# Weight-sum DMAs of the first down product: eight of 48 asked for two tiles earlier, and a lower rate behind the half-size tiles

## The chip, the core and the metric

The kernel runs on one core of a Trainium2 chip. The metric is the time of one execution on the device in microseconds (us); with several runs of a kernel, their median. All data are float32. TensorE multiplies matrices into PSUM banks, VectorE and ScalarE do the elementwise work, GpSimd (POOL in the profile) does little but issue DMAs that copy or accumulate in DRAM, and SyncE (SP) issues the DMAs that load weights. Each of the two has a DMA queue of its own in the profile (q0 for GpSimd, q1 for SyncE), and both move their bytes with the same 16 DMA engines.

## What is computed

One layer of a streaming encoder on 512 tokens of width 1024:

```python
x = x + 0.5 * swiglu_ffn(rmsnorm(x, g1), w_gate1, w_up1, w_down1)   # hidden width 2816
x = x + hybrid_mixer(rmsnorm(x, gm), ...)                           # attention and pooling
x = x + 0.5 * swiglu_ffn(rmsnorm(x, g2), w_gate2, w_up2, w_down2)
x = rmsnorm(x, gf)

def swiglu_ffn(x, w_gate, w_up, w_down):
    return (silu(x @ w_gate) * (x @ w_up)) @ w_down
```

The change lies in the first feed-forward block, whose two halves are called the up stage (gate and up products and SiLU) and the down product.

## The kernel before

**Precision.** Each float32 operand is split into a high and a low part (`split`, L128; ScalarE writes the high part, VectorE the low), and each product is three TensorE products (`mm3`, L173 to L178).

**The up stage** (`ffn_up`, L383) works through 22 feature tiles of 128 hidden features, numbered here in their order, 0 to 21. Tiles 0 to 4 (`PLAIN` = 5) are full-size: each takes 2 x 8 products of 128x512, with weights loaded by `weights` (L163). Tiles 0 and 1 are made together from the first four loads (L406 to L420) and then evacuated from PSUM by `evacuate` (L393), which scales, applies SiLU, multiplies gate and up into the activations and returns the tile `sg` that held the SiLU. Tiles 2 and 3 follow in the loop at L492, and tile 4 at L506 to L528.

Tiles 5 to 21 are half-size (loop at L550): a Strassen-like scheme replaces eight half-size products by seven, each of 4 x 3 TensorE products of 128x256. It needs sums and differences of weight blocks, which VectorE makes (`sum13`, `sum24`, `low...`) and ScalarE splits (`high...`, L444). From L548 the order of TensorE, VectorE, ScalarE and SyncE is as written in the code (`manual_schedule`); before that a scheduler places the instructions. In tile n, SyncE fetches the weights of tile n + 2 with two DMAs of 512 KB (`fetch`, L431: L436 and L437, tensor `in_wA`), into one of two raw buffers, which VectorE's last reader of tile n has just freed. Behind that ScalarE splits the first block of tile n + 1 (`high11`, L574, executed at L444), which the second DMA (L437) of the fetch made one tile earlier brings. Behind it, in ScalarE's order, stands the copy of a PSUM bank (`copy(z[:, HT:], up_hi, -1.0)`, L580, executed at L540) that must be done before TensorE writes that bank again (L584).

**The weight sums.** The down product uses the same scheme, and its sums of weight blocks (T1 to T4, for 6 groups of rows) are made in DRAM ahead of time by GpSimd's queue: `Down.steps` (L646) lists 48 DMAs, 24 that copy a block to `wsum` (from the weights `in_wB`, or from another `wsum`) and 24 that accumulate a second block onto it. Most of them move 512 KB, those of the last group 256 KB. An accumulation can only be issued when the copy beneath it has landed, a copy from another `wsum` only when that one is complete. They are issued in the order of the list.

**What paces them.** `make_sums(after, n)` (L669) takes the next steps from the list. It copies one column of the tile `after` to a mark (L675), which makes GpSimd wait until that tile is written, and then issues the steps (L677). The number is taken from `rates`, given where `down1` is made (L800 to L801): four behind each of tiles 2, 3 and 4, three behind each of the next six, two behind each of the next nine. It is called in the loop at L501, at L528, and once in each half-size tile (L586, behind VectorE's L585). The GpSimd part of the code is in written order as well, except that marks can be placed ahead of steps that still wait.

The down product reads the sums from L704 on, first at 216.6 us of the profiled execution. The second feed-forward block uses the same functions with `loaded=True`, its own object `down2` and no rates.

Of the kernel before, what the change touches and what calls it, by code (L numbers as in the profile page):

```python
# [23 lines left out]
KH = KF // 2  # L24
# [15 lines left out]
PLAIN = 5  # L40
# [13 lines left out]
def layer(  # L54
# [50 lines left out]
    def temp(dtype=F32):  # L105
        return tpool.tile([P, S], dtype, tag="t", name=name("t"))

    def bank(tag="mm", bufs=4):
        return ps.tile([P, S], F32, tag=tag, name=name(tag), bufs=bufs)
# [63 lines left out]
    def mm3(acc, a, b, start, stop, further=False):  # L173

        more = dict(skip_group_check=True) if further else {}
        nc.tensor.matmul(acc, a[0], b[0], start=start, stop=False, **more)  # L176
        nc.tensor.matmul(acc, a[0], b[1], start=False, stop=False, **more)  # L177
        nc.tensor.matmul(acc, a[1], b[0], start=False, stop=stop, **more)  # L178

    def cut(pair, lo, n):  # L180
        if isinstance(pair[0], list):
            pair, lo = [z[lo // S] for z in pair], lo % S
        return pair[0][:, lo : lo + n], pair[1][:, lo : lo + n]
# [199 lines left out]
    def ffn_up(norm, wA, down, loaded):  # L383
# [9 lines left out]
        def evacuate(f, gate, up):  # L393
            g = temp()
            nc.vector.tensor_tensor(g, gate, norm.rb, op=ALU.mult)
            sg = temp()
            nc.scalar.activation(sg, g, AF.Silu)

            nc.vector.tensor_tensor(sg, sg, norm.rb, op=ALU.mult)
            down.place(f, up, sg)  # L400
            down.sums(f)
            return sg

        consts = constants()
        first = [bank() for _ in range(4)]
        for kp in range(KD // 2):  # L406
# [10 lines left out]
            for kk in range(2):  # L417
                k = 2 * kp + kk
                for j in range(4):
                    mm3(first[j], cut(w, (kk * 4 + j) * P, P), norm.h[k], k == 0, k == KD - 1)  # L420
        evacuate(0, first[0], first[1])
        evacuate(1, first[2], first[3])
        aside = [
            down.pool.tile([P, 6 * groups[g][1] * HT], F32, tag=f"acts{groups[g][0]}", name=name("aside"))
            for g in (G - 3, G - 2, G - 1)
# [80 lines left out]
        n, f = PLAIN - 1, down.order[PLAIN - 1]  # L506
# [41 lines left out]
        with tc.manual_schedule(engines={E.PE, E.DVE, E.Activation, E.SP}):  # L548
            last_silu = last_place = last_sums = nothing
            for n in range(PLAIN, KF):  # L550
                f = down.order[n]
                acc, up_lo, up_hi = bank()[:, :HT], bank()[:, :HT], abank()[:, :HT]
                u, z, sg = temp(), temp(), temp()
# [238 lines left out]
    def block2(i, g):  # L792
# [4 lines left out]
    KPS = (2, 3, 0, 1)  # L797
    order1 = [0, 1, KH, KH + 1] + [f + KH * j for f in range(2, KH) for j in range(2)]
    down1 = Down(
        order1, lambda f: (f % KH, f // KH), block1, [4] * (PLAIN - 2) + [3] * 6 + [2] * 9  # L800
    )  # L801
    down2 = Down(list(range(KF)), lambda f: (f // 2, f % 2), block2)

    with tc.tile_pool(name="act1", bufs=1, reuse_waits="tile") as apool:
        down1.begin(apool)
        ffn_up(n1, wA1, down1, loaded=False)
        p1, p5, p6 = whole(bank), whole(bank), whole(abank)

# [615 lines left out]
    with tc.tile_pool(name="act2", bufs=1, reuse_waits="tile") as apool:  # L1424
        down2.begin(apool)

        for half in range(2):
            for t in range(NT):
# [6 lines left out]
                nc.scalar.copy(z, tp)  # L1435
                nc.sync.dma_start(x_d[half * NT + t], z)
        ffn_up(n3, wA2, down2, loaded=True)
        xt = [hpool.tile([P, S], F32, tag="h", name=name("xt")) for _ in range(2 * NT)]
        rooms.extend((xpool, f"x{i}", 1, 2 * S) for i in range(KD // 2))
# [212 lines left out]
```

## Time and profile before

| what | value |
|---|---|
| median of 3 runs | 864.71 us (863.97 to 865.85) |
| profiled execution, time on the device | 865.0 us |
| its span from first to last instruction | 863.2 us |
| granted TensorE clock | 0.998 |
| GpSimd's DMA queue q0 | 22656 packets, 46.14 MB, 24.7% of the DMA engines' time |
| SyncE's DMA queue q1 | 49088 packets, 110.93 MB, 36.8% |
| up stage of the first block: full-size tiles | about 5 to 65 us |
| up stage of the first block: half-size tiles | about 65 to 236 us |

How to read it: the page gives busy times of each engine over the whole span and in slices; a row of the table by stage gives them for one stretch, with the granted clock, the busy share of the DMA engines (which can exceed 1, as packets overlap) and the GB/s. A row of a timeline gives the start, the duration, the engine, the source line (often that of a helper), the operation and its tiles; a bracket at the end tells how long the engine stood idle just before it, and what ended that idle time. Times are from the start of the span.

### The profile page before, as it was taken

What the parts mean: (1) busy time and instruction counts of PE and PEld (TensorE: products, weight loads), DVE (VectorE), ACT (ScalarE), POOL (GpSimd) and SP (SyncE); (2) the same over time, 40 slices, a digit from 0 to 9 for tenths busy, and PEclk for the clock granted to TensorE, in tenths of its full rate; (3) what the DMA queues carried; (4) which work ended last, traced back from release to release, by engine and by line L of the source; (5) the groups of instructions that cost most, each with busy time, mean ns of one, the idle gap of its engine ahead of it and who ended that gap; (6) DMA issues with size and microseconds to landing.
All of it is one profiled execution on the core that took longest, in us unless ns stands there. A gap on an engine that the chain in (4) does not pass through costs nothing.

```text
span 863.2 us, 14110 instructions
## 1 busy us (share of the span) xinstructions
PE 848.8 (98%) x5296; PEld 757.5 (88%) x5296; DVE 708.3 (82%) x1115; ACT 501.1 (58%) x859; POOL 120.1 (14%) x196
## 2 busy tenths in 40 slices
PE   9999999999999999989999999999999999999996
PEld 7889999999988888867878788889999999988885
DVE  7999898898897769685878667969888898887896
ACT  7445555555676556548647756445555555566573
POOL 0124322222000000120011000102112111122000
PEclk9999999999999999999999999999999999999999
DMA  8199998877576764322212026248778778899832
GB/s 291 57 285 248 293 277 207 202 206 165 144 242 204 254 212 136 97 86 85 75 57 90 25 73 244 80 140 228 212 231 202 189 199 209 251 328 341 274 109 98
DMA packets 72244, 158.50 MB, mean 184 GB/s; under 512 B 6112, under 2 KB 29168, under 8 KB 71792
## 3 DMA queue, kind: packets, MB, share of 16 engines
q1 hardware_dynamic: 49088, 110.93, 36.8%
q0 software_dynamic: 22656, 46.14, 24.7%
q8 instruction: 41, 0.67, 0.3%
q10 hardware_dynamic: 432, 0.54, 0.2%
q14 instruction: 27, 0.22, 0.1%
HBM read 153.38 MB, written 50.34 MB: 236 GB/s over the span
## 4 chain that ended last, share of the span: by engine, by line
PE 91%; DVE 3%; DMA 2%; ACT 2%; issue 1%; SPq 0%; ACTq 0%; DVEq 0%
PE mm L176 22%; PE mm L177 21%; PE mm L178 21%; PE a L176 7%; PE a L177 7%; PE a L178 7%; DMA raw<-in_wA_dram 2%; PE a L1172 1%; PE a L1226 1%; PE a L1214 1%; DVE t L1093 1%; DVE wlo L449 1%; ACT prob L1153 1%; PE a L211 0%; PE a L1431 0%
## 5 line engine op out<-in xcount | busy, mean ns | idle before, releaser
L132 DVE TENSOR_TENSOR wlo<-raw,whi 128x1024 fp32r<-128x1024 f32 (+2 forms) x115 | 125.0, 1096 | 20.7 <-ACT whi L131 20.4
L131 ACT CAST whi<-raw 128x1024 fp32r<-128x1024 f32 (+2 forms) x115 | 106.9, 944 | 57.7 <-PE mm L177 15.5
L177 PE MATMUL mm<-ha,whi 128*128 128x256 f32 x408 | 115.6, 283 | 0.0
L178 PE MATMUL mm<-ha,wlo 128*128 128x256 f32 x408 | 115.0, 282 | 0.0
L176 PE MATMUL mm<-ha,whi 128*128 128x256 f32 x408 | 115.0, 282 | 0.0
L540 ACT ACTIVATE t<-mm 128x256 f32<-128x256 f32 x102 | 39.2, 384 | 121.5 <-PE mm L178 120.8
L449 DVE TENSOR_TENSOR wlo<-wsum,whi 128x1024 fp32r<-128x1024 f32 x68 | 83.0, 1220 | 14.1 <-ACT whi L444 14.1
L178 PEld LDWEIGHTS mm<-ha,wlo 128*128 128x128 f32 x408 | 77.4, 190 | 0.0
L176 PEld LDWEIGHTS mm<-ha,whi 128*128 128x128 f32 x408 | 77.2, 189 | 0.1
L177 PEld LDWEIGHTS mm<-ha,whi 128*128 128x128 f32 x408 | 77.2, 189 | 0.1
L176 PE MATMUL mm<-hhi,whi 128*128 128x512 f32 x192 | 76.0, 399 | 0.0
L177 PE MATMUL mm<-hlo,whi 128*128 128x512 f32 x192 | 75.7, 395 | 0.0
L178 PE MATMUL mm<-hhi,wlo 128*128 128x512 f32 x192 | 74.8, 392 | 0.0
L677 POOL DMA_DIRECT2D wsum<-in_wB_dram x72 | 70.4, 1147 | 11.7 <-issue 8.5
L444 ACT CAST whi<-wsum 128x1024 fp32r<-128x1024 f32 x68 | 67.9, 1048 | 4.1 <-PE mm L177 3.9
L177 PE MATMUL mm<-wlo,ah 128*128 128x512 f32 x176 | 68.6, 390 | 0.0
L178 PE MATMUL mm<-whi,ah 128*128 128x512 f32 x176 | 68.5, 389 | 0.0
L176 PE MATMUL mm<-whi,ah 128*128 128x512 f32 x176 | 68.4, 390 | 0.0
L675 POOL COPY mark<-t 128x1 f32<-128x1 f32 x40 | 15.1, 377 | 382.1 <-DVE t L585 228.0
L449 DVE TENSOR_TENSOR wlo<-raw,whi 128x512 fp32r<-128x512 f32 x68 | 62.5, 951 | 3.4 <-ACT whi L444 3.4
L444 ACT CAST whi<-raw 128x512 fp32r<-128x512 f32 x68 | 56.3, 828 | 11.4 <-DMA raw<-in_wA_dram 6.9
L132 DVE TENSOR_TENSOR ah<-acts,ah 128x512 fp32r<-128x512 f32 (+1 forms) x72 | 45.7, 641 | 14.5 <-ACT ah L131 14.2
(211 smaller groups left out, 2381.5 us busy)
## 6 DMA issues: line engine op xcount, KB each, us to landing
raw<-in_wA_dram SPq DMA_DIRECT2D x87, 512.0 KB, 5.5
wsum<-in_wB_dram POOLq DMA_DIRECT2D x60, 512.0 KB, 7.7
raw<-wsum SPq DMA_DIRECT2D x40, 512.0 KB, 4.4
raw<-in_wB_dram SPq DMA_DIRECT2D x30, 512.0 KB, 4.7
wsum<-wsum POOLq DMA_DIRECT2D x20, 512.0 KB, 5.8
x<-in_xT_dram SPq DMA_DIRECT2D x16, 256.0 KB, 5.7
raw<-in_wQK_dram SPq DMA_DIRECT2D x8, 512.0 KB, 3.5
raw<-in_wO_dram SPq DMA_DIRECT2D x8, 512.0 KB, 3.4
```

The lines of the kernel that those rows point to most:

```text
L131: nc.scalar.copy(hi, src)
L132: nc.vector.tensor_tensor(lo, src, hi.bitcast(F32), op=ALU.subtract)
L176: nc.tensor.matmul(acc, a[0], b[0], start=start, stop=False, **more)
L177: nc.tensor.matmul(acc, a[0], b[1], start=False, stop=False, **more)
L178: nc.tensor.matmul(acc, a[1], b[0], start=False, stop=stop, **more)
L444: nc.scalar.copy(hi, src)
L449: nc.vector.tensor_tensor(lo, src, hi.bitcast(F32), op=ALU.subtract)
L540: nc.scalar.activation(dst, src, AF.Copy, scale=scale)
L675: nc.gpsimd.tensor_copy(mark, after[:, 0:1])
L677: nc.gpsimd.dma_start(self.rows(i, g), self.rows(self.terms[i][at], g), **(dict(accum_op=ALU.add) if at else {}),)
L1093: nc.vector.tensor_tensor(q3, q3, rs[:, t, :].unsqueeze(2).to_broadcast([P, 8, HD]), op=ALU.mult)
L1153: nc.scalar.activation(p, p, AF.Copy, scale=rt)
```

## The change

The steps of the first down product are also asked for behind tiles 0 and 1, four each, and the rates become four behind each of tiles 0, 1 and 2, three behind each of tiles 3 and 4, and two behind each of the next fifteen (half-size) tiles. The sum is 48 as before. The second block is not touched, since `loaded` is true there.

```diff
-        evacuate(0, first[0], first[1])
-        evacuate(1, first[2], first[3])
+        for f in range(2):
+            sg = evacuate(f, *first[2 * f : 2 * f + 2])
+            if not loaded:
+                down.make_sums(sg, 2)
...
     down1 = Down(
-        order1, lambda f: (f % KH, f // KH), block1, [4] * (PLAIN - 2) + [3] * 6 + [2] * 9
+        order1, lambda f: (f % KH, f // KH), block1, [4] * 3 + [3] * (PLAIN - 3) + [2] * 15
     )
```

The functions `evacuate` and `make_sums` themselves are unchanged.

## The prediction, made before the changed kernel was run

> **What bounds the kernel now.** I read the first part of the page, then the table by stage around the change, then who waits for whom there, and last the rows of ScalarE and of the queues in order of time. The page:
>
> ```profile
> span 863.2 us, 14110 instructions
> PE 848.8 (98%) x5296; PEld 757.5 (88%) x5296; DVE 708.3 (82%) x1115; ACT 501.1 (58%) x859; POOL 120.1 (14%) x196
> ```
>
> TensorE is busy for 98% of the span, so a change that moves only DMAs can win only where TensorE stands still for a DMA. The busy time by stage (PE, PEld, DVE, ACT, POOL, granted clock, DMA share, GB/s) shows where that could be:
>
> ```profile
> 30.00:41.00 11.00, 11.00 (x50) 9.13 (x49) 11.00 (x16) 4.12 (x6) 2.25 (x2) 1.00 0.00 0
> 41.00:66.00 25.00, 25.00 (x126) 21.30 (x126) 23.99 (x33) 13.39 (x20) 8.42 (x10) 1.00 0.89 253
> 77.00:87.00 10.00, 9.74 (x83) 9.54 (x81) 7.56 (x10) 4.98 (x9) 3.09 (x4) 1.00 1.09 314
> 87.00:97.00 10.00, 9.54 (x81) 9.55 (x82) 8.70 (x12) 5.87 (x12) 4.97 (x6) 1.00 1.11 318
> ```
>
> From 30 to 41 us no byte is moved, from 41 us on the DMA engines are full, and TensorE loses its first time behind them, after 77 us. The waits from 60 to 125 us (us in total, times, longest) name the chain:
>
> ```profile
> ACT whi L444 <- DMA raw<-in_wA_dram: 4.7, 3, 2.2
> PEld a L176 <- ACT t L540: 1.5, 2, 0.9
> ```
>
> ScalarE waits for the second weight DMA of a half-size tile (L437) to split its first block (L444, `high11`). Behind it in ScalarE's queue stands the copy L540 that frees the PSUM bank `up_hi`, and TensorE waits for that copy. How much that costs is read from the cadence. The last L540 copy of each tile, and the L444 that waits:
>
> ```profile
> 69.67 0.39 ACT L540 ACTIVATE t<-mm 128x256 f32<-128x256 f32 x1 [2.45 <-PE mm L178]
> 79.64 0.39 ACT L540 ACTIVATE t<-mm 128x256 f32<-128x256 f32 x1 [2.45 <-PE mm L178]
> 86.50 0.62 ACT L444 CAST whi<-raw 128x512 fp32r<-128x512 f32 x1 [2.17 <-DMA raw<-in_wA_dram]
> 90.56 0.38 ACT L540 ACTIVATE t<-mm 128x256 f32<-128x256 f32 x1 [2.88 <-PE mm L178]
> 96.05 0.62 ACT L444 CAST whi<-raw 128x512 fp32r<-128x512 f32 x1 [0.77 <-DMA raw<-in_wA_dram]
> 100.50 0.39 ACT L540 ACTIVATE t<-mm 128x256 f32<-128x256 f32 x1 [2.45 <-PE mm L178]
> 107.00 0.62 ACT L444 CAST whi<-raw 128x512 fp32r<-128x512 f32 x1 [1.75 <-DMA raw<-in_wA_dram]
> 111.09 0.39 ACT L540 ACTIVATE t<-mm 128x256 f32<-128x256 f32 x1 [2.92 <-PE mm L178]
> 150.99 0.39 ACT L540 ACTIVATE t<-mm 128x256 f32<-128x256 f32 x1 [2.45 <-PE mm L178]
> 220.80 0.39 ACT L540 ACTIVATE t<-mm 128x256 f32<-128x256 f32 x1 [2.45 <-PE mm L178]
> ```
>
> Undisturbed, a tile takes (220.80 - 150.99) / 7 = 9.97 us. The tile that ends at 90.56 took 10.92 (0.95 lost), the one at 111.09 took 10.59 (0.62 lost), the two beside them 9.97 and 9.94. Late fetches cost 0.95 + 0.62 = 1.57 us here. That is the ceiling of what this change can win: 0.18% of 865.0. Everywhere else that the change touches, TensorE is already without gaps.
>
> **What moves.** The 48 weight-sum DMAs of the first down product keep their order. Asked for so far, behind full-size tiles 0 to 4 and then half-size tiles 5, 6, 7: before 0, 0, 4, 8, 12, 15, 18, 21; after 4, 8, 12, 15, 18, 20, 22, 24. From tile 10 on both stand at 30 and go on in twos. In the compiled order TensorE, VectorE, ScalarE and SyncE keep every instruction in place; GpSimd gets two more mark copies (of 128 elements), and VectorE and ScalarE get one more wait on GpSimd each, for a temporary that tile 4 takes over from a marked one. Tile 4's temporaries are written after 62 us and these marks are read before 40 us, so I cost the waits at nothing; they would count only if GpSimd ran over 20 us late, and its waits below are of 3 us.
>
> The mark copies stand in a stretch where VectorE has no idle time. A copy there and the queue's first DMAs:
>
> ```profile
> 29.89 0.68 DVE L399 TENSOR_TENSOR t<-t,rb 128x512 f32<-128x512 f32 x1
> 38.75 2.25 POOL L675 COPY mark<-t 128x1 f32<-128x1 f32 x1 [36.95 <-DVE t L399]
> 36.87 1.22 DVE L343 TENSOR_TENSOR aside<-aside,aside 128x1024 f32<-128x1024 f32 x1
> 39.74 1.22 DVE L343 TENSOR_TENSOR aside<-aside 128x1024 f32<-128x1024 f32 x1
> 45.70 1.97 POOL L677 DMA_DIRECT2D wsum<-in_wB_dram  x2 [3.09 <-DMA wsum<-in_wB_dram]
> 54.05 0.51 POOL L677 DMA_DIRECT2D wsum<-wsum  x1 [2.51 <-DMA wsum<-in_wB_dram]
> 61.64 0.69 DVE L132 TENSOR_TENSOR ha<-aside,ha 128x512 fp32r<-128x512 f32 x1 [0.67 <-PE mm L177]
> ```
>
> Tile 0's mark becomes ready at 30.57 instead of 38.69 for tile 2's, so the queue starts about 8 us earlier. GpSimd pays at most 2 x 2.25 us more, which nobody but the queue waits for. If a mark held VectorE for its whole 2.25 us, VectorE would have the 0.67 us idle at 61.64 against it; between 0 and 2 x 2.25 us I take 0, since the same addition (L343) takes 1.22 us before the mark at 36.87 and beside it at 39.74. Each accumulation waits until the copy beneath it has landed (the 3.09 and 2.51 us), so the early start is partly spent in waiting.
>
> **Work in the two queues.** Mean rates: accumulations alone (73 to 76 us), copies alone (43 to 45), a weight fetch alone (129.2 to 131.4):
>
> ```profile
> DMA packets 578, 0.59 MB, mean 197 GB/s; under 512 B 18, under 2 KB 576, under 8 KB 577
> DMA packets 190, 0.71 MB, mean 356 GB/s; under 512 B 16, under 2 KB 16, under 8 KB 190
> DMA packets 280, 0.63 MB, mean 285 GB/s; under 512 B 17, under 2 KB 17, under 8 KB 280
> ```
>
> A step of 0.52 MB is 2.66 us as an accumulation and 1.47 us as a copy; a tile's 1.05 MB fetch is 3.7 us. Three steps per half-size tile are on average 6.2 us, with the fetch 9.9 us in a tile of 9.97: a backlog never clears. Two steps are 4.1 + 3.7 = 7.8 us: 2.1 us of a backlog go away per tile. That is the gain. The fetches and what they met:
>
> ```profile
> 43.19 0.61 SPq L437 DMA_DIRECT2D raw<-in_wA_dram  x1
> 66.83 0.55 SPq L437 DMA_DIRECT2D raw<-in_wA_dram  x1
> 74.25 0.61 ACT L444 CAST whi<-raw 128x512 fp32r<-128x512 f32 x1
> 75.86 10.56 DMA raw<-in_wA_dram
> 96.74 10.18 DMA raw<-in_wA_dram
> DMA to landing us min/median/max: 4.4/6.4/10.6
> ```
>
> The two that cost time took 10.56 and 10.18 us; the median of L437 is 6.4. Taking off the losses, a fetch may take 10.56 - 0.95 = 9.61 or 10.18 - 0.62 = 9.56 us before TensorE stops. One has less: tile 7's fetch, issued at 66.83. Its deadline is one tile ahead of tile 8's, 75.86 + 9.61 - 9.97 = 75.50, so 8.67 us. Before, it met an empty queue (ScalarE at 74.25 did not wait). After, 15 steps lie ahead of it, 9 copies and 6 accumulations, 13.2 + 16.0 us, and two fetches, 7.4 us: 36.6 us of work, with 33 us from the first packets at about 34 us, less the waits on landings. So 4 us or more are left over when it starts, and tile 4's three steps (two copies and a half-size one, 3.7 us) come in beside it. Its time lies between the median 6.4 and 10.56; I take 9.5, nearer to the loaded end, since its queue is loaded. That stops TensorE for 9.5 - 8.67 = 0.8 us at about 76 us. The stop gives the next fetch 0.8 us more room (9.6 + 0.8 = 10.4 against the loaded 10.2): no loss. The backlog shrinks by 2.1 us per tile, so tile 10's fetch, which cost 0.62, meets a nearly empty queue.
>
> The Trainium skill (DMA: Bandwidth & Descriptors, "Queues, rings and completion order") says that a DMA engine takes turns between its queue rows, packet by packet. The 10.56 and 10.18 us beside a lightly loaded 6.4 agree: what slows a fetch would be whether the other queue has anything, not how much. That speaks against this change: by it the sum would be that of case C below.
>
> **Sum.** -1.57 (stops removed) + 0.8 (new stop) = -0.8 us: the 865.0 of the profiled execution (its span is 863.2, and 1.8 us lie around it) becomes 864.2. The median, 864.71, lies 0.3 below that execution, within the spread of the three runs (863.97 to 865.85); from it the sum gives 863.9. I predict 864.0, between the two. A difference under 0.2% (1.7 us) is about what a measurement of this kernel cannot tell from none.
>
> **Rivals.**
> A: every fetch lands in time (tile 7's under 8.67 us). For: two steps need only 7.8 of 9.97 us. Against: the load before 66 us. -1.57, 863.1 from the median. Chance 0.24.
> B, my forecast: one smaller stop, earlier. Gain 0.3 to 1.3. Chance 0.40.
> C: the change does not do what it says, the stops only move one tile ahead. Where the fetch takes turns with a queue that is not empty, fetches 7 to 9 take 10.2 us and more, however few steps stand behind: 10.2 - 8.67 = 1.5 us, as much as goes. Change 0, 864.7 (-0.3 to +0.5). Chance 0.22. The rule of the Trainium skill quoted above would have this as long as the other queue has work.
> D, slower: tile 5's fetch, issued at 43.19, now falls among accumulations. ScalarE's split that waits for it starts at 50.41, 7.2 us after the issue; at 10.2 us it starts at 53.4, and VectorE's half, now at 52.30, right behind it at 54.0, 1.7 later. VectorE's only reserve up to 66 us is the 0.67 at 61.64, so it frees the raw buffer 1.0 us later and tile 7's fetch leaves at 67.9; at 10.2 it lands at 78.1, 2.6 behind its deadline. 2.6 - 1.57 is +1.0 us: 865.7. At 11.4 us, two thirds of an accumulation more, it would be 866.9. It decides once tile 5's fetch takes over 8.5 us (52.30 less the split's 0.62 is 51.7), and shows in full once it takes over 9.2:
>
> ```profile
> 50.41 0.62 ACT L444 CAST whi<-raw 128x512 fp32r<-128x512 f32 x1 [2.03 <-DMA raw<-in_wA_dram]
> 52.30 0.68 DVE L449 TENSOR_TENSOR wlo<-raw,whi 128x512 fp32r<-128x512 f32 x1
> ```
>
> Chance 0.14.
>
> **Numbers.** Faster by over 0.2% needs 863.0 or less, below A's 863.1, so only a part of A, where the median hid longer stops than the profiled execution: 0.08. Slower by over 0.2% needs 866.4, the upper half of D and a little of C: 0.09. Within: 0.83. The range goes from A (863.1) to D (865.7) with the sum's rounding: 863.0 to 865.8.
>
> **What would show it.** Right: weight-sum DMAs between 32 and 43 us; no L444 wait over 1 us after 95 us; half-size tiles of 9.97 us from the third on; one tile of about 10.8 that ends near 80 us. Wrong: all tiles 9.97 (A), two or three tiles over 10.4 (C), VectorE's L449 at 52.30 moved past 53 (D). A time outside the range would mean that the change reaches a stage where I saw no cover missing.

## The result

| | the changed kernel | the kernel before, same chips |
|---|---|---|
| median of 21 runs each | 867.58 us (865.03 to 869.79) | 865.05 us (863.97 to 866.78) |
| ratio of the two | 1.0024 (95% interval 1.0016 to 1.0032) | |
| profiled execution, its span | 869.31 us, 867.5 us | 865.0 us, 863.2 us |
| granted clock of the profiled execution | 0.996 | 0.998 |

The changed kernel is slower, by about 2 us; the forecast was 864.0 in a range of 863.0 to 865.8, no difference or a slight gain. The page of the changed kernel (two lines are added in its code, so L449 is L451, L540 is L542, L675 is L677):

```profile
span 867.5 us, 14116 instructions
PE 850.4 (98%) x5296; PEld 759.0 (87%) x5296; DVE 708.0 (82%) x1115; ACT 500.9 (58%) x859; POOL 124.2 (14%) x198
```

Of the 4.3 us that the span grew, TensorE's busy time has 1.6 with the same 5296 matmuls, and idle time the rest. A larger busy time for the same instructions asks for a look at the clock. The table by stage of the changed kernel (columns as before: PE, PEld, DVE, ACT, POOL, granted clock, DMA share, GB/s):

```profile
30.00:41.00 11.00, 11.00 (x50) 9.12 (x49) 11.00 (x16) 4.01 (x5) 4.47 (x6) 1.00 0.56 135
41.00:66.00 25.00, 24.79 (x121) 20.82 (x119) 22.16 (x31) 11.61 (x18) 15.38 (x13) 1.00 1.01 278
77.00:87.00 10.00, 7.77 (x53) 7.57 (x53) 5.21 (x10) 2.65 (x6) 2.91 (x4) 0.83 1.09 301
...
82.00:88.00 6.00, 6.00 (x41) 6.00 (x41) 4.45 (x7) 2.47 (x4) 1.34 (x2) 0.75 1.16 258
...
98.00:108.00 10.00, 10.00 (x86) 10.00 (x85) 9.51 (x16) 5.60 (x11) 1.17 (x3) 1.00 0.55 200
```

The DMAs do start early (share 0.56 from 30 to 41 us instead of 0.00), and from 98 us on the load is light, as intended. Between the two, TensorE loses over 2 us from 77 to 87 us, and from 82 to 88 us the granted clock is 0.75 on average: in the trace's record of the clock it is 0.5 for 3.413 us from 81.64 on. TensorE's rows there show both, a stop and then matmuls of 0.41 us that take 0.28 at full clock:

```profile
65.51 0.28 PE L178 MATMUL a<-xa,wlo 128*128 128x256 f32 x1
67.09 0.39 PE L176 MATMUL mm<-xa,whi 128*128 128x256 f32 x1 [1.29 <-ACT t L542]
...
78.36 0.28 PE L178 MATMUL mm<-xa,wlo 128*128 128x256 f32 x1
80.87 0.38 PE L176 MATMUL a<-ha,whi 128*128 128x256 f32 x1 [2.23 <-ACT t L542]
...
82.34 0.41 PE L176 MATMUL a<-ha,whi 128*128 128x256 f32 x1
...
85.09 0.28 PE L177 MATMUL mm<-ha,whi 128*128 128x256 f32 x1
```

Matmuls start 0.12 us apart when nothing stops them, so the first stop costs 67.09 - 65.51 - 0.12 = 1.46 us and the second 80.87 - 78.36 - 0.12 = 2.39. (The idle time in the bracket is 0.28 less than the distance of the starts, for a matmul is counted busy for 0.28. The expectations below give stops by the distance of the starts.) ScalarE's rows, the split that waits for a fetch and the last copy of each tile:

```profile
54.78 0.62 ACT L446 CAST whi<-raw 128x512 fp32r<-128x512 f32 x1 [5.99 <-PE mm L178]
...
71.57 0.39 ACT L542 ACTIVATE t<-mm 128x256 f32<-128x256 f32 x1 [2.40 <-PE mm L178]
...
79.92 0.62 ACT L446 CAST whi<-raw 128x512 fp32r<-128x512 f32 x1 [3.69 <-DMA raw<-in_wA_dram]
80.72 0.38 ACT L542 ACTIVATE t<-mm 128x256 f32<-128x256 f32 x1
85.53 0.38 ACT L542 ACTIVATE t<-mm 128x256 f32<-128x256 f32 x1 [4.44 <-PE mm L178]
...
95.47 0.39 ACT L542 ACTIVATE t<-mm 128x256 f32<-128x256 f32 x1 [2.45 <-PE mm L178]
...
105.44 0.39 ACT L542 ACTIVATE t<-mm 128x256 f32<-128x256 f32 x1 [2.45 <-PE mm L178]
...
115.42 0.39 ACT L542 ACTIVATE t<-mm 128x256 f32<-128x256 f32 x1 [2.45 <-PE mm L178]
```

By the cadence of the prediction, the tile that ends at 85.53 took 13.96 us, 3.99 over the usual 9.97: 2.39 of the stop and 1.60 of the half clock. All later tiles take 9.94 to 9.98. So the stops of before (1.57) are gone, and the account of the profiled execution is -1.57 + 1.46 + 2.39 + 1.60 = +3.9, beside some 0.4 that it was already behind at 43 us (tile 5's fetch issued at 43.60 instead of 43.19), together the 4.3.

What was late? The chain of work (start, duration, what) of the changed kernel in this stretch, and GpSimd's rows:

```profile
64.41 0.69 DVE t L395
...
68.59 0.35 SPq L438
68.99 10.85 DMA raw<-in_wA_dram
79.96 0.48 issue
80.44 0.39 ACT t L542
```

```profile
36.01 1.97 POOL L679 DMA_DIRECT2D wsum<-in_wB_dram  x2 [2.45 <-DMA wsum<-in_wB_dram]
42.41 0.51 POOL L679 DMA_DIRECT2D wsum<-wsum  x1 [4.43 <-DMA wsum<-in_wB_dram]
...
52.98 0.52 POOL L679 DMA_DIRECT2D wsum<-wsum  x1 [4.66 <-DMA wsum<-in_wB_dram]
...
59.01 0.50 POOL L679 DMA_DIRECT2D wsum<-wsum  x1 [3.54 <-DMA wsum<-in_wB_dram]
59.50 5.04 POOL L677 COPY mark<-t 128x1 f32<-128x1 f32 x1
64.48 3.12 POOL L679 DMA_DIRECT2D wsum<-in_wB_dram  x3
```

Two fetches are late. Tile 5's, issued at 43.60, lands after 11.1 us, and ScalarE splits only at 54.78 (50.41 before; the row names a matmul as what ended the idle time, but the landing, at 54.7, came last). VectorE's part follows (55.44 instead of 52.30), VectorE reaches tile 4's evacuation late (L395 at 64.41 instead of 62.25), and TensorE stops for the bank at 65.5 us. That also delays tile 7's fetch, from 66.83 to 68.99, and it takes 10.85 us: the second stop. GpSimd has spent 2.45 + 4.43 + 4.66 + 3.54 = 15.1 us waiting for its own steps to land, and 5.04 us in one mark, so with all its early start it issues steps 13 to 15 (a copy and two accumulations) only from 64.48 on, right ahead of that fetch.

What the second fetch met shows in the DMA queues. The view of the first 3.6 us after its first DMA was issued (68.59 to 72.19; packets, MB, share of the 16 engines' time) has GpSimd's queue alone:

```profile
q0 software_dynamic: 538, 0.54, 107.7%
```

The first weight packet of the fetch moves 3.64 us after the issue. In the kernel before it moves after 0.97 us, and the first 3.6 us (66.43 to 70.03) belong to the fetch:

```profile
q1 hardware_dynamic: 283, 0.81, 64.2%
q0 software_dynamic: 17, 0.01, 4.7%
```

Not every execution looks like this one. Of the 21 runs, 14 have a mean clock of 0.996 or less and a median of 868.30 us; the other seven have 865.36, hardly more than before. (In the fourteen profiled executions of this document, the six with a stretch at half clock have a mean clock of 0.994 to 0.996, the eight without one 0.998.) The loss sits in executions with a stretch at half clock. It is more than that stretch alone: the two groups lie 2.9 us apart, the stretch costs 1.60, so the stop itself must be shorter in the seven; no trace of one was kept.

### The profile page after: what moved, and what is told of

Read it like the earlier page. It is cut to its first block, busy times and chain, and to the rows that moved or that the text cites. A ratio compares the mean times of both kernels' runs of the same rounds, so it can differ in the third digit from the quotient of the medians.

```text
span 867.5 us, 14116 instructions
## 1 busy us (share of the span) xinstructions
PE 850.4 (98%) x5296; PEld 759.0 (87%) x5296; DVE 708.0 (82%) x1115; ACT 500.9 (58%) x859; POOL 124.2 (14%) x198
## 4 chain that ended last, share of the span: by engine, by line
PE 92%; DVE 3%; DMA 2%; ACT 2%; issue 0%; SPq 0%; ACTq 0%; DVEq 0%
PE mm L176 22%; PE mm L177 22%; PE mm L178 22%; PE a L177 8%; PE a L176 8%; PE a L178 8%; DMA raw<-in_wA_dram 1%; PE a L1174 1%; PE a L1228 1%; PE a L1216 1%; DMA x<-in_xT_dram 1%; DVE t L1095 1%; ACT prob L1155 1%; PE a L1433 0%; PE a L1103 0%
## 5 line engine op out<-in xcount | busy, mean ns | idle before, releaser
L542 ACT ACTIVATE t<-mm 128x256 f32<-128x256 f32 x102 | 39.3, 385 | 123.8 <-PE mm L178 123.2
L451 DVE TENSOR_TENSOR wlo<-wsum,whi 128x1024 fp32r<-128x1024 f32 x68 | 82.9, 1220 | 14.4 <-ACT whi L446 14.4
L677 POOL COPY mark<-t 128x1 f32<-128x1 f32 x42 | 20.9, 497 | 384.4 <-DVE t L587 232.6
L451 DVE TENSOR_TENSOR wlo<-raw,whi 128x512 fp32r<-128x512 f32 x68 | 62.2, 950 | 5.9 <-ACT whi L446 5.9
```

The source lines that it names most:

```text
L451: nc.vector.tensor_tensor(lo, src, hi.bitcast(F32), op=ALU.subtract)
L542: nc.scalar.activation(dst, src, AF.Copy, scale=scale)
L677: nc.gpsimd.tensor_copy(mark, after[:, 0:1])
```

## The experiments

Two questions were open. **Which late fetch matters**: tile 5's, which falls among accumulations because eight steps come earlier (the collision theory), or tile 7's, which meets a queue that is still at work, whatever made it so? And **is the half clock a consequence of the stop alone** (the clock theory), or of the DMA load? The changes of `rates` are given against the kernel before, [4, 4, 4] + [3] * 6 + [2] * 9 behind tiles 2 to 19. Where tiles 0 and 1 have entries, the two added calls of `make_sums` are there. Each result is the kernel's median, that of the kernel before on the same chip, and the ratio with its 95% interval.

### No early steps, the low rate alone

To keep the sum at 48, tiles 2 and 3 ask for five steps each, so ten steps are asked for up to tile 3, where the kernel before has eight.

```diff
-[4] * (PLAIN - 2) + [3] * 6 + [2] * 9
+[5, 5, 4] + [2] * 17
```

> The kernel before with only the lower rate: nothing behind tiles 0 and 1, then 5, 5 and 4 steps behind tiles 2, 3 and 4, and two behind each half-size tile. Collision theory (the steps asked for behind tiles 0 and 1 lie in the queue when tile 5's weight fetch starts at 43 us, and that alone makes it slower): tile 5's fetch takes 7 to 9 us, no stop of TensorE at 65 us, at most one stop of up to 1.5 us near 76 to 88 us, none after 95 us; 863.5 to 865.5 us. Rate theory (the lower rates move the stops forward and make them longer): stops at 65 and 78 us as in the changed kernel, about 867 us.

868.24 us against 865.39, 1.0025 (1.0015 to 1.0035): as slow as the changed kernel, with no step before tile 2. In its trace tile 5's fetch takes 6.4 us and there is no stop at 65 us. The chain, TensorE and the table by stage:

```profile
66.69 11.20 DMA raw<-in_wA_dram
```

```profile
78.93 0.41 PE L176 MATMUL a<-ha,whi 128*128 128x256 f32 x1 [2.30 <-ACT t L540]
```

```profile
79.00:84.00 5.00, 5.00 (x30) 5.00 (x31) 3.93 (x7) 0.56 (x3) 0.18 (x1) 0.66 1.07 302
```

Tile 7's fetch left on time (66.69) and took 11.20 us; the stop, and 3.413 us at half clock behind it, are those of the changed kernel. The collision theory falls as the cause: tile 7's fetch brings the long stop and the half clock by itself. The rate theory had the time about right, but its stop at 65 us did not come. A part of this kernel's loss is something else, a stop of 1.10 us idle at 247 us in the down product (the last steps come two tiles later here). What stands ahead of the fetch are steps 9 and 10, both accumulations. Here they are issued at 63.18, in the kernel before at 66.39 together with step 11, beside the fetch (66.43):

```profile
63.18 2.41 POOL L677 DMA_DIRECT2D wsum<-in_wB_dram  x2
```

```profile
66.39 3.14 POOL L677 DMA_DIRECT2D wsum<-in_wB_dram  x3
```

As in the changed kernel, only GpSimd's queue moves packets in the first 3.6 us after the issue (444 of them, 0.45 MB), and the fetch's first one moves after 4.00 us.

### The early steps, with the old rate behind them

```diff
-[4] * (PLAIN - 2) + [3] * 6 + [2] * 9
+[4] * 5 + [3] * 6 + [2] * 5
```

> The other half alone: four steps behind each of tiles 0 to 4, then the rates of before (three behind each of six half-size tiles, then two). Collision theory: the stops at 65 and 78 us of the changed kernel return, of 1 to 2.5 us each, with the clock at half for some 3.4 us after the longer one, and a further stop may come later, since three steps per tile clear no backlog; 867 to 870 us. Rate theory: with the higher rates back it is as before, 864.5 to 865.5 us.

873.15 us against 865.39, 1.0088 (1.0075 to 1.0102), the slowest of all schedules, beyond both expectations, and without a stop at 65 us. TensorE's row and the table by stage:

```profile
80.10 0.58 PE L176 MATMUL a<-ha,whi 128*128 128x256 f32 x1 [3.30 <-ACT t L542]
```

```profile
80.00:87.00 7.00, 6.90 (x35) 6.90 (x36) 4.55 (x9) 1.70 (x5) 1.73 (x4) 0.57 1.18 249
```

One stop of 3.30 us idle at tile 7's fetch (12.20 us), then half clock for 6.827 us, twice as long; three more stops (the largest 2.6 us from start to start) follow up to 166 us, each behind a late fetch. That three steps per tile leave no room for them is argued, not tested by itself.

### The two added marks without steps

```diff
-[4] * (PLAIN - 2) + [3] * 6 + [2] * 9
+[0, 0] + [4] * (PLAIN - 2) + [3] * 6 + [2] * 9
```

> The kernel before with two more mark copies, behind tiles 0 and 1, and no step asked for there; all steps as before. Collision theory: nothing changes, 864.6 to 865.5 us, VectorE's operation at 52.30 us stays within 0.5 us. Mark theory (the marks themselves, or the waits that VectorE and ScalarE get on GpSimd, hold VectorE up): it moves past 53 us, and the time is over 866.5 us.

865.51 us against 865.39, 1.001 (0.9997 to 1.0022): the marks, and the waits that they bring, cost nothing that can be seen, and VectorE's operation of 52.30 stands at 52.04.

### Early steps, but less work ahead of tile 7's fetch

```diff
-[4] * (PLAIN - 2) + [3] * 6 + [2] * 9
+[4, 0, 0, 5, 3] + [2] * 13 + [3] * 2 + [2] * 2
```

> Steps placed so that the queue is empty when tile 5's fetch starts: four behind tile 0 (they have landed by about 43 us), none behind tiles 1 and 2, five behind tile 3, three behind tile 4, two behind each half-size tile but two late ones with three. Collision theory: tile 5's fetch takes under 7 us, no stop at 65 us, at most one stop of up to 1 us near 76 us, none after 90 us, clock never at half before the end; 863.2 to 864.8 us. Rate theory or mark theory: no better than the changed kernel, about 867 us.

864.73 us against 865.39, 0.9993 (0.9985 to 1.0002). This keeps four early steps and leaves the queue free while tile 5's fetch runs. No stop from 30 to 240 us; one of 1.0 us from start to start at 242 us, where the down product waits for sums that now come late. Every mean clock is 0.997 or more.

The next one changes less. It keeps the twelve steps behind tiles 0 to 2 exactly, and takes away those behind tile 3 (one of tile 4's three as well):

```diff
-[4] * (PLAIN - 2) + [3] * 6 + [2] * 9
+[4, 4, 4, 0, 2] + [2] * 17
```

> The changed kernel's twelve early steps behind tiles 0, 1 and 2 as they are, but none behind tile 3, two behind tile 4, and two behind each half-size tile. Tile-5 theory (the early steps make tile 5's fetch late, and VectorE carries that on): as the changed kernel, tile 5's fetch over 10 us and stops at 65 and 78 us, 867 to 869 us. Tile-7 theory (what costs is the work, accumulations above all, that lies in the queue when tile 7's fetch leaves at 66 to 69 us, since that fetch has only 8.7 us; the lateness of tile 5 adds at most 1.4 us): tile 5's fetch is still over 10 us and a stop of up to 1.4 us at 65 us may stay, but tile 7's fetch takes under 8.5 us, the stop near 78 us is under 1 us, the clock stays full; 864.5 to 866 us.

864.46 us against 865.5, 0.9992 (0.9984 to 1.0001). ScalarE's split behind tile 7's fetch, GpSimd, and the table by stage:

```profile
74.51 0.61 ACT L446 CAST whi<-raw 128x512 fp32r<-128x512 f32 x1
```

```profile
59.40 0.50 POOL L679 DMA_DIRECT2D wsum<-wsum  x1 [4.23 <-DVE ha L132]
...
66.64 1.92 POOL L679 DMA_DIRECT2D wsum<-in_wB_dram  x2
```

```profile
41.00:66.00 25.00, 25.00 (x126) 21.27 (x125) 24.00 (x34) 13.52 (x21) 8.64 (x11) 1.00 1.02 281
66.00:78.00 12.00, 12.00 (x103) 12.00 (x103) 11.73 (x17) 6.08 (x12) 4.75 (x6) 1.00 0.97 240
78.00:88.00 10.00, 10.00 (x86) 10.00 (x85) 9.10 (x13) 5.58 (x10) 1.45 (x3) 1.00 0.70 249
```

The split starts at 74.51 without a wait, 7.4 us after the fetch was issued (67.08), and TensorE is without gaps there; a stop of 1.02 us idle comes at 243 us, in the down product. Tile 5's fetch was expected to take over 10 us and took 6.4, so this trace says nothing against the tile-5 theory; the first experiment does. Up to tile 4 this kernel has asked for 14 steps, exactly as many as the first experiment, which lost 2.85 us. The difference is when they run: here step 12 is issued at 59.40 and the queue is idle when the fetch leaves; there steps were issued at 62.69 and 63.18, two accumulations among them, and stood ahead of it.

Two more put the late steps back in time for the down product:

```diff
-[4] * (PLAIN - 2) + [3] * 6 + [2] * 9
+[4, 0, 0, 5, 3] + [2] + [2, 3] * 6 + [2] * 2
```

> The placement with an empty queue at 43 us (4, 0, 0, 5, 3 behind tiles 0 to 4) with the 48 steps done by tile 19 as before (2, then six times 2 and 3 in turn, then 2, 2 behind the half-size tiles), so that the down product no longer waits for late sums. Tile-7 theory: no stop over 0.5 us between 30 and 300 us, 863.3 to 864.5 us, 0.1 to 0.2% below the kernel before. If three steps in a tile by themselves bring late fetches back: stops of 0.5 to 1 us in some of tiles 7 to 17, 864.5 to 866.

864.24 us against 865.5, 0.9993 (0.9984 to 1.0001). The profiled execution, 863.57 us, has no stop from 30 to 358 us. The stage of tile 7's fetch:

```profile
66.00:78.00 12.00, 12.00 (x104) 12.00 (x103) 11.71 (x18) 6.07 (x11) 4.81 (x7) 1.00 1.10 291
```

The stops that the prediction priced at 1.57 us, its ceiling, are gone in this trace, and the interval still includes 1: no schedule is shown to beat the kernel before. One accumulation (step 9) was under way here when tile 7's fetch left; the split behind the fetch waited 0.29 us, which cost TensorE nothing.

```diff
-[4] * (PLAIN - 2) + [3] * 6 + [2] * 9
+[4, 4, 4, 0, 2] + [2, 3] * 4 + [2] * 7
```

> The placement with twelve steps behind tiles 0 to 2, none behind tile 3 and two behind tile 4, with the rest (2 and 3 in turn four times, then 2) done by tile 19 as before, so that the down product does not wait near 243 us. Tile-7 theory: all fetches from tile 7 on under 9.5 us, no stop over 0.5 us between 30 and 300 us, 863.2 to 864.3 us. If more steps per tile bring late fetches back: stops of 0.5 to 1 us between 85 and 180 us, 864.3 to 866 us.

865.6 us against 865.72, 0.9997 (0.9987 to 1.0007): a miss, at the time that its rival had named. Its trace has a stop at 156 us, 0.9 from start to start, and in its profiled execution 3.413 us at half clock at 488 us, behind two stops in the attention part (0.84 and 1.39 us from start to start) that the kernel before has as well. What the median lost was not pursued.

### Stops without any DMA

To separate the clock from the DMAs, the kernel before got added copies on ScalarE in half-size tile 12, ahead of the copy that frees the bank; they write a tile that is overwritten later. Their times include the added work.

```diff
+                if n == 12 and not loaded:
+                    for _ in range(7):
+                        nc.scalar.copy(sg, raws[n + 1][:, :S])
...
                 copy(z[:, HT:], up_hi, -1.0)
```

> The kernel before with seven more copies of 128x512 (0.53 us each) on ScalarE in one half-size tile (tile 12, near 140 us), ahead of the copy that TensorE waits for; no DMA is touched. Clock theory (a stop of TensorE of about 2.4 us, whatever its cause, is followed by some 3.4 us at half clock, which costs 1.7 us more): a stop of 2.2 to 2.7 us and in the same execution 3.4 us at half clock; +4 us where that happens, +2.4 where it doesn't, median 867 to 869.5. Rival (the half clock comes from the load on the DMA engines or from chance): the stop alone, +2.4 us, about 867.5, and the clock full.

> The same with four copies. Clock theory: a stop of 0.7 to 1.2 us, the clock full, +0.5 to +1.2 us, 865.5 to 866.5 us, with a narrow spread. Rival that any stop costs half clock: +2.5 us or more.

> The kernel before with ten more copies on ScalarE in tile 12, no DMA touched. Clock theory: a stop of 4.4 to 4.9 us, followed by 3.4 or 6.8 us at half clock in nearly every execution, 870.5 to 873.5 us. Rival (half clock needs something else than the stop): the stop alone, 869.5 to 870.5 us, clock full in the profile.

> The kernel before with six added ScalarE copies of 128x512 in half-size tile 12 (nothing of the output changes, no DMA is touched). Four copies stopped TensorE for 1.25 us, seven for 3.2, ten for 5.16, so 0.65 us for one copy and 2.55 us for six, about the 2.4 us that the changed kernel stops for its tile 7. Clock theory (a stop of that length is followed, in most executions, by 3.41 us at half clock, worth 1.7 us): the median is 869 to 870, some 3.7 to 4 over the kernel before, with most mean clocks at 0.996 or less. Rival (it needs a full DMA load or a stop of over 3 us): every mean clock at 0.997 or more and a median of 867.3 to 868.2.

| copies | median, before | ratio | stop, idle us | runs with mean clock 0.996 or less |
|---|---|---|---|---|
| 4 | 866.61, 865.5 | 1.0017 (1.0009 to 1.0026) | 0.97 | 0 of 12 |
| 6 | 868.68, 865.73 | 1.0035 (1.0022 to 1.0047) | 2.27 | 5 of 6 |
| 7 | 869.72, 865.5 | 1.0052 (1.004 to 1.0064) | 2.92 | 4 of 5 |
| 10 | 873.07, 865.72 | 1.0083 (1.0065 to 1.0101) | 4.88 | 4 of 4 |

Six copies make the stop of the changed kernel at a place where fetches are on time. TensorE's row and the stage behind it:

```profile
140.53 0.39 PE L176 MATMUL a<-ha,whi 128*128 128x256 f32 x1 [2.27 <-ACT t L540]
```

```profile
141.00:146.00 5.00, 5.00 (x32) 5.00 (x32) 1.23 (x3) 0.81 (x2) 1.76 (x3) 0.68 0.42 161
```

Half clock for 3.413 us follows here at a DMA share of 0.42, and with ten copies for 6.827 us at a share of 0.22:

```profile
142.00:149.00 7.00, 5.33 (x25) 5.33 (x26) 0.42 (x1) 1.83 (x5) 1.43 (x3) 0.51 0.22 87
```

The clock theory holds: a stop brings it without any late DMA. Of the kernel before on the same chips, none of 29 runs (with four and seven copies), none of 10 (six) and 3 of 23 (ten) have so low a mean clock. The times fit less well: four and seven copies came out 0.1 and 0.2 us above their ranges, and six copies 0.3 below theirs, 2.95 over the kernel before, where the stop (2.43 by the distance of the starts, less 0.12) and 1.60 of half clock would make 4.0. So the price of 1.60 us rests on the profiled execution of the changed kernel, not on these medians. The one execution with seven copies that kept its full clock is the profiled one (868.06 us against a median of 869.8 for the other four), with a stop of 2.92 us idle. So a stop of that length does not always bring it; the last section says what decides.

### The copy ahead of the split

If ScalarE's copy of `up_hi` did not stand behind the split, would tile 7's late fetch still stop TensorE? The changed kernel, with that copy moved ahead of `high11` in the first block:

```diff
+                if not loaded:
+                    copy(z[:, HT:], up_hi, -1.0)
                 high11(n + 1)
...
-                copy(z[:, HT:], up_hi, -1.0)
+                if loaded:
+                    copy(z[:, HT:], up_hi, -1.0)
```

> The changed kernel, its DMAs untouched, with one instruction moved in the half-size tiles of the first block: ScalarE copies the PSUM bank that TensorE waits for ahead of the split that waits for the fetch. Tile-7 theory (the late fetch reaches TensorE only because that copy stands behind the waiting split in ScalarE's order): tile 7's fetch still takes 9 to 11 us, but the stop near 78 us is gone or under 0.8 us, and the clock stays full; 864 to 866 us; VectorE may now be what is late, by up to 1 us. Rival (TensorE needs the late weights themselves, or VectorE behind them): the stop stays over 2 us, 867 to 869 us.

866.04 us against 865.72, 1.0005 (0.9994 to 1.0016): no slower than the kernel before, as far as this can tell. The stop was expected to shrink below 0.8 us and did not. TensorE, then ScalarE, then the fetch in the chain:

```profile
80.20 0.38 PE L176 MATMUL mm<-ha,whi 128*128 128x256 f32 x1 [1.89 <-ACT t L542]
```

```profile
75.59 0.39 ACT L542 ACTIVATE t<-a 128x256 f32<-128x256 f32 x1 [1.09 <-PE a L178]
79.25 0.62 ACT L446 CAST whi<-raw 128x512 fp32r<-128x512 f32 x1 [3.27 <-DMA raw<-in_wA_dram]
79.77 0.38 ACT L542 ACTIVATE t<-mm 128x256 f32<-128x256 f32 x1
```

```profile
66.97 12.20 DMA raw<-in_wA_dram
```

The copy of `up_hi` (75.59) is out of the way, but the next copy (79.77, of the bank `acc`) still stands behind the split, and TensorE stops for that one, one product later. A product is 12 matmuls of 0.12 us, 1.4 us, and that much is won: with a fetch that landed at the same time (79.06 in the second experiment, 79.17 here), the stop is 2.05 us instead of 3.46. The fetch here took 12.20 us, though it left on time: in this execution tile 5's fetch landed after 6.6 us, with the same DMAs. GpSimd issues its steps 5 and 6 at 43.30 and 43.79 here, behind that fetch (42.90); in the changed kernel's profiled execution they came at 42.41 and 42.91, ahead of it (43.18). So tile 5's part in the changed kernel differs from run to run, and tile 7's does not need it. The profiled execution, with its stop of 1.89 us idle, kept the full clock; 3 of 12 runs have a mean clock of 0.996 or less, but so have 3 of 23 runs of the kernel before on this chip.

## Why the prediction was wrong

- **What it said would show it**: DMAs from 32 us on, no late split after 95 us and tiles of 9.97 us behind the stop all came; the one long tile near 80 us took 13.96 us instead of about 10.8.
- **The ceiling** of 1.57 us fits: the later stops went in the changed kernel, and in the trace of one quiet schedule with no new one. Their worth stays below what the medians can show.
- **The marks and waits at nothing** were right (1.001, interval with 1). GpSimd paid up to 5.04 us for one mark, more than the 2.25 that bounded it, and nobody but the queue waited. That mark is not the cause: in the last experiment it took 2.02 us, steps 13 to 15 were issued from 60.25 on, and tile 7's fetch was as late.
- **The step that failed** is "so 4 us or more are left over when it starts ... I take 9.5": the size of tile 7's fetch. The working filled the time with bytes at mean rates and put the waits on landings into "or more". GpSimd waited 15.1 us of the 33 up to there, three whole steps were issued at 64.48, and the fetch took 10.85 us (11.20, 12.20 and 12.20 in three kernels where it left on time), more than the 10.56 that bounded it. The stop is 2.39 us where 0.8 was forecast. In the profiled execution the fetch also left 2.16 us late, but that hardly adds to this stop, since TensorE was late by then too. The deadline was right: 75.50 + 0.41 + 1.46 = 77.37, and the fetch landed at 79.84, 2.47 late; in the first experiment it landed 2.53 late for a stop of 2.46. The kernel before already showed waits longer than the 3 us that the working took: 12.25 us in all up to 63.20, with this one:

```profile
63.20 0.50 POOL L677 DMA_DIRECT2D wsum<-wsum  x1 [6.65 <-DMA wsum<-in_wB_dram]
```

- **Rival D** had tile 5's fetch land late, and its sign came: VectorE's L451 at 55.44, past the 53 that it named. It priced only the delay of tile 7's fetch; TensorE also stopped by itself at 65.5 us (1.46). But the first experiment shows the same stop at tile 7 and the same half clock without it, and the last the same late fetch, so D was a part of this execution, not the cause. (The step in D from 10.2 to 11.4 us is 0.45 of an accumulation's 2.66, not two thirds.)
- **The missing term** is the clock. Forecast and rivals priced a stop at its own length; behind the stop of 2.39 us came 1.60 us more. That took the time beyond the forecasts of all four cases, and the range ended at D's 865.7, short of the 866.9 that D itself named for a fetch of 11.4 us.
- **Case C** said that fetches 7 to 9 take 10.2 us and more however few steps stand behind. Fetch 7 did, and later ones did not; with an idle queue at its start it took at most 7.4 us with two steps issued beside it. By the Trainium skill's rule quoted there (DMA: Bandwidth & Descriptors, "Queues, rings and completion order"), the fetch would have its turns as soon as both queues have work; the packets of the trace show none for 3.64 us, and the measurement decides. How many of the trace's packets one turn of that rule covers, no run shows.

So it matters which queue is first. In the four traces with a late fetch 7 (the changed kernel, the first, second and last experiments), two accumulations had been issued ahead of it, and its first packet moves 3.63 to 4.00 us after the issue. In the other ten traces none or one had been, and it moves after 0.97 to 1.44 us (at 1.44, with four added copies, a stop of 0.79 us idle still follows at 77 us). What stays open is why the fetch's packets wait so long behind an accumulation that is under way, and whether copies in its place would hold them as long: no run exchanged the two.

## What to carry to other kernels

Spreading DMAs by a mean rate is not enough: look at what each transfer with a short deadline meets when it leaves, and count the issuing engine's own waits before you call a queue drained. A stop of TensorE is to be priced with what follows it, here 1.6 us more behind 2.4, so one long stop can cost more than several short ones that lie far apart. A copy moved ahead of a late split buys the time up to the next copy behind it, here 1.4 us, and no more.

## What the runs showed of the hardware

- Half clock (0.5, matmuls of 0.41 us instead of 0.28) followed idle times of TensorE of 2.23, 2.30 and 2.27 us for 3.413 us, and of 3.30 and 4.88 us for 6.827 us. By the mean clock it came after 0.97 us in none of 12 runs and after 2.27 in 5 of 6. It is not certain at these lengths: in the slowest schedule a later stop of 2.31 us idle (at 143 us) passed at full clock, and so did the one of 2.92 us.
- The Trainium skill (TensorE: Matmul & The Clock Gate, "Part 1: The HAM clock gate (the "warmup" mystery)") gives a free-running window of 3413 ns and a half clock after at least one idle window. The lengths agree; the idle times of 2.2 to 2.3 us are shorter than a window, and here the measurement decides.
- Where a stop falls decides. In the six traces with half clock it begins a whole number of times 3.413 us after the record of the clock begins (22, 22, 22, 40, 40 and 141 times), so each trace can be cut into such windows. Between 20 and 850 us of the fourteen traces, each window with 2.23 us or more of TensorE's idle time was followed by half clock (five windows), and each with 1.65 or less, entered at full clock, by full clock; at 1.68 it was half clock once and full clock twice. The stop of 2.92 us lay across an edge, 1.56 on one side and 1.36 on the other, the one of 2.31 with 0.66 and 1.65, the one of 1.89 in the last experiment with 0.68 and 1.21. Two short stops in one window did bring it (0.56 and 1.12, at 488 us in one placement). So about half a window of idle time within one window suffices in these traces, and whether a stop of 2 to 3 us costs the 1.6 us more is partly luck.
- A mark, a copy of 128 elements on GpSimd, took 5.04 us at 59.50, where VectorE worked without a pause, and 0.18 us beside less dense work:

```profile
94.97 0.18 POOL L677 COPY mark<-t 128x1 f32<-128x1 f32 x1 [5.88 <-DVE t L587]
```
